# A two-layer mixer and feed-forward step on one core: the modulation vectors as 32-column float32 products on TensorE inside the mixers

## The chip, the cores and the metric

The kernel runs on one NeuronCore of a Trainium2 chip. The metric is the device time of one execution in microseconds; the kernel before takes 1740.79 us (median of three runs, 1739.17 to 1743.87). Engines are named as in the profile: PE is TensorE's matrix product, PEld its weight load, DVE VectorE, ACT ScalarE, POOL GpSimd, SP the engine whose queue issues most loads.

## The reference

One step of a hybrid backbone with two layers over 640 tokens (512 latent, 128 context) of width 1024. Cut to what matters here:

```python
def trunk_layer(x, mod, s0, prm, l, pool_seg):
    sh1, sc1, g1, sh2, sc2, g2 = jnp.split(mod, 6, axis=-1)
    h = rmsnorm(x, prm['norm1_g'][l]) * (1 + sc1) + sh1
    cols = jnp.einsum('bnd,de->bne', h, prm['w_in'][l])
    ...                       # gated DeltaNet, chunked MLP, pooling
    x = x + g1 * mix
    h = rmsnorm(x, prm['norm2_g'][l]) * (1 + sc2) + sh2
    gate, up = jnp.split(jnp.einsum('bnd,df->bnf', h, prm['w_gu'][l]), 2, axis=-1)
    x = x + g2 * jnp.einsum('bnf,fd->bnd', silu(gate) * up, prm['w_down'][l])

# for the context tokens (c_ctx) and for the latent tokens (c), in each layer:
mod = jnp.einsum('bd,de->be', jax.nn.silu(c), w_mod[l]) + b_mod[l]     # 6144 numbers
```

The part that changes is `mod`: for each of two layers a product of two vectors of 1024 numbers (context and latent) with a matrix of 1024 x 6144 float32 numbers, 25 MB a layer.

## The kernel before

Tokens lie in the free dimension, features on the 128 partitions. Every large product runs in float32r with both operands split in a high and a low part, so one block of 128 x 128 weights takes three matmuls of 320 (or 322) columns: `xhi,wh`, `xlo,wh` and `xhi,wl` (`mm3`, line 117 through the helper `mm`). A weight tile `w` of 8 row blocks comes by SP, is split by ACT (line 322), DVE (line 122) and POOL (line 326), and serves two halves of 320 tokens (`gemm_xs`, or `gemm_act` for the output and down projections).

A layer has four stages. **The mixer**: 22 weight tiles of the input projection, and between them the DeltaNet of two pairs of heads, each with short convolutions, decay matrices (`prep`), an inverse by substitution (`inverse`, whose 15 steps are products with `selr`, each waiting for DVE) and a scan over five chunks (`chain`, products on `R` and `S` with DVE steps between). **The output projection**: 8 tiles, each followed by the residual `x` and the scaled split `xhi`, `xlo` for the next norm. **The feed-forward part**: 22 pairs of gate and up products in three pieces, each piece followed by 8 tiles of the down projection.

**The modulation.** The first two sixths of layer 0 (shift and scale of the first norm) are made at the start by `first_mod` on PE: `sc` holds the two condition vectors as 32 columns per row block, and four row blocks run side by side on different column groups of the array (`tile_position=(0, 32 g)`), each a float32 product of 512 moving columns of `w_mod`. Four transposes and a reduction then give the columns. The other ten sixths of both layers are 160 **steps** of 512 columns x 128 rows each (`pump_`): DVE multiplies and adds for the one condition (line 125, `ma<-wm,sc,ma`), ACT multiplies for the other (line 150, `wm<-wm,sc`) and POOL adds (line 282). After 8 steps `mod_sums` adds over the partitions: with 8 transposes on PE and two DVE reductions in layer 0's mixer and output projection, with DVE transposes and four tiny products (`ms,quarters`) in the feed-forward part. Steps are put behind halves of products: by the table `PUMPS` in layer 0's mixer (32 of them by its end), one behind each half in the output projection and in the feed-forward part. All 160 are done by 802 us; layer 1 has none in its output projection or its feed-forward part, and none in its mixer. The load of a step (256 KB) is issued three steps ahead (`WM` = 3) by SP.

**The order.** Instructions have priorities in the order of the program, with offsets from the table `PRI` (`at(...)`); a scheduler makes from these a fixed order on each engine, and each engine runs its own order strictly. PSUM tiles for the small products (`md`) come from a ring of two, shared by the modulation, the transposes of `row_sums` and others.

Of the kernel before, what the change touches and what calls it, by code (L numbers as in the profile page):

```python
# [16 lines left out]
D = 1024  # L17
# [14 lines left out]
POUT = 1  # L32
# steps of the modulation after each half of a product, by branch
PUMPS = {'log0': (0, 0), 'k00': (0, 0), 'q00': (1, 2), 'sgu0': (1, 1), 'z0': (0, 1), 'v10': (1, 1), 'q10': (0, 0), 'v00': (1, 0), 'k10': (0, 1), 'pool0': (1, 0)}
# [11 lines left out]
def host_constants():  # L46
# [10 lines left out]
    # from here on: not kept on chip as they are  # L57
# [34 lines left out]
def tile_hybrid_step(ctx: ExitStack, tc: tile.TileContext,  # L92
# [59 lines left out]
    class at:  # L152
        """the instructions inside come that much earlier in the order of issue"""
# [23 lines left out]
    def in_turn(key, ins):  # L177
        """instructions of one kind in the order of the program"""
# [29 lines left out]
    quarters = const.tile([P, 32], F32, name="quarters")  # L208
# [10 lines left out]
    # steps: 512 columns x 128 rows of w_mod; a step's load is issued some steps ahead of its arithmetic  # L219
    SIXTHS = [(0, 2), (0, 4), (0, 3), (0, 5), (1, 1), (1, 0), (1, 2), (1, 4), (1, 3), (1, 5)]  # L220
    steps = [(l, w * D + c0, k) for l, w in SIXTHS for c0 in (0, 512) for k in range(KT)]
    ps_ = {"i": 0, "j": 0, "ma": None, "wm": {}, "due": None, "at": "mix0"}

    def mod_sums(l, c0, ma):
        t0 = c0 // P
        if ps_["at"] != "ffn0":
            for s in range(2):
                pt = md()
                for cb in range(4):
                    nc.tensor.transpose(pt[:, cb * P:(cb + 1) * P], ma[:, s, cb * P:(cb + 1) * P], ident)  # L230
                m = mod[:, l, s, t0:t0 + 4]
                nc.vector.tensor_reduce(m, pt.rearrange("p (c n) -> p c n", c=4), op=ADD, axis=AX.X)
                tt(m, m, bmod[:, l, t0:t0 + 4], ADD)
            mod_scales(l, c0)
            return
        # sums over the 32 rows of each quarter, then over the quarters
        ms = sm.tile([P, 2, 16], F32, tag="ms", name="ms", bufs=1)
        for s in range(2):
            pt = md()
            nc.vector.transpose(pt, ma[:, s])  # L240
            nc.vector.tensor_reduce(ms[:, s], pt.rearrange("p (c n) -> p c n", n=32), op=ADD, axis=AX.X)
        pt = md()
        for a in range(4):
            mm(pt[32 * a:32 * a + 32, 0:8], quarters, ms.rearrange("p s (t a) -> p a s t", a=4)[:, a], True, True, tile_position=(0, 32 * a))
        tt(mod[:, l, :, t0:t0 + 4], pt[:, 0:8].rearrange("p (s t) -> p s t", s=2),
           bmod[:, l, t0:t0 + 4].unsqueeze(1).to_broadcast([P, 2, 4]), ADD)
        mod_scales(l, c0)
# [5 lines left out]
    def pump(n=1):  # L253
        with at("pump"):
            pump_(n)

    def pump_(n):
        for _ in range(n):
            if ps_["due"] is not None:
                mod_sums(*ps_["due"])  # L260
                ps_["due"] = None
            i = ps_["i"]
            if i >= len(steps):
                return
            while ps_["j"] < min(len(steps), i + WM):
                l, c0, k = steps[ps_["j"]]
                wm = wp.tile([P, 512], F32, tag="wm", name="wm", bufs=WM)
                nc.sync.dma_start(wm, w_mod[l, k * P:(k + 1) * P, c0:c0 + 512])
                ps_["wm"][ps_["j"]] = wm
                ps_["j"] += 1  # L270
            l, c0, k = steps[i]
            wm = ps_["wm"].pop(i)
            if k == 0:
                ps_["ma"] = sm.tile([P, 2, 512], F32, tag="ma", name="ma", bufs=1)
            ma = ps_["ma"]
            if k == 0:
                behind_recent("v", ts, ma[:, 0], wm, sc[:, k, 0:1], None, MUL)
                behind_recent("a", times, f"pump{ps_['at']}", ma[:, 1], wm, sc[:, k, 1:2], "a")
            else:
# [3 lines left out]
            if k == KT - 1:  # L283
                ps_["due"] = (l, c0, ma)
            ps_["i"] += 1

    def pump_to(l, w):
        """until that sixth of the modulation is there"""
        n = 2 * KT * (SIXTHS.index((l, w)) + 1)
        while ps_["i"] < n:  # L290
            pump()
        if ps_["i"] == n and ps_["due"] is not None:
            mod_sums(*ps_["due"])
            ps_["due"] = None

# [1 line left out]
    def wload(parts, kn, n):  # L297
        """parts: [(dram [rows, n], k0, kn)] -> [P, kn, n]"""
# [7 lines left out]
    def wsplit(v):  # L306
        """hi, lo as blocks [P, n]"""
# [32 lines left out]
    def mmk(o, wb, k, xk, sl):  # L340
        """one k block of the products with the scaled residual; 16 columns: hi and lo in one operand"""
# [47 lines left out]
    class Norm:  # L389
        """scaled residual split in two, and the row statistics of the plain one."""  # L390
# [33 lines left out]
        def rstd(self, after=None):  # L424
            """per row: [row in chunk, chunk]"""
# [30 lines left out]
    wsp = tc.alloc_tile_pool(name="wsh", bufs=1, side="right")  # L456
    with tc.tile_pool(name="xin", bufs=1) as xp:
# [27 lines left out]
        def first_w(pool, j, c0, kp=KT):  # L485
            """512 columns of w_mod; the row blocks from kp on in the tiles of the later steps"""
# [950 lines left out]
```

## Time and profile before

| | |
|---|---|
| median of three runs | 1740.79 us (1739.17 to 1743.87) |
| profiled execution, first to last instruction | 1737.7 us |
| PE busy, PEld busy | 1666.4 us (96%), 1603.2 us (92%) |
| DVE, ACT, POOL busy | 1155.2 us (66%), 761.1 us (44%), 585.3 us (34%) |
| mean granted PE clock | 0.987 of full |

The page gives no other time of the profiled execution than this span. Busy times of PE are to be read with care: a matmul of 320 columns is shown with 0.31 us, while in dense stretches the next one starts 0.15 us after it, so short waits disappear behind the modelled ends.

### The profile page before, as it was taken

How to read it: one execution, taken by the hardware profiler on the slowest of the kernel's cores; microseconds unless marked ns; L12 is line 12 of the kernel's file. 1: busy time of each engine (PE TensorE's matmuls, PEld its weight loads, DVE VectorE, ACT ScalarE, POOL GpSimd, SP SyncE). 2: the span in 40 equal slices, each digit the busy share in tenths (PEclk: the TensorE clock that was granted, in tenths of full speed). 3: DMA queues.
4: the chain of work that ended last, by engine and by line, in shares of the span. 5: the costliest groups of instructions: out<-in, count | busy, mean ns of one | idle time of the engine just before them, and what ended most of it. 6: DMA issues, size and time to landing. Idle time of an engine off the chain costs nothing.

```text
span 1737.7 us, 33153 instructions
## 1 busy us (share of the span) xinstructions
PE 1666.4 (96%) x12952; PEld 1603.2 (92%) x12952; DVE 1155.2 (66%) x2462; ACT 761.1 (44%) x1564; POOL 585.3 (34%) x578
## 2 busy tenths in 40 slices
PE   6999999998899999999999999999999999999997
PEld 4788989988899999999998899999999999999997
DVE  6698688799888688877467777675544434433454
ACT  4557765554444344434246656543322212321232
POOL 3342330367645454554164112013411221222110
PEclk8999999999999999999999999999999999999999
DMA  9431231444444544453241211113222222222221
GB/s 316 143 98 57 68 99 29 150 127 139 145 141 141 154 137 143 143 158 103 62 144 52 62 38 50 37 51 126 83 73 74 79 79 74 74 73 73 74 85 61
DMA packets 243379, 174.34 MB, mean 100 GB/s; under 512 B 10006, under 2 KB 212376, under 8 KB 243224
## 3 DMA queue, kind: packets, MB, share of 16 engines
q1 hardware_dynamic: 231888, 157.44, 29.8%
q10 hardware_dynamic: 10184, 12.29, 2.2%
q0 software_dynamic: 1152, 2.51, 0.4%
q8 instruction: 102, 1.67, 0.4%
q14 instruction: 53, 0.43, 0.1%
HBM read 163.29 MB, written 8.91 MB: 99 GB/s over the span
## 4 chain that ended last, share of the span: by engine, by line
PE 53%; DVE 3%; ACT 1%; issue 1%; POOL 0%; DMA 0%; DVEq 0%; POOLq 0%; ACTq 0%
PE acc L117 47%; PE dl L117 5%; DVE wl L122 0%; PE md L117 0%; DMA w<-in_w_down_dram 0%; PE dl L1379 0%; DVE cv L125 0%; POOL guh L830 0%; PE md L760 0%; DVE yt L125 0%; DVE st L125 0%; DVE Z L122 0%; ACT wh L322 0%; ACT MT L945 0%; DVE SI L122 0%
## 5 line engine op out<-in xcount | busy, mean ns | idle before, releaser
L117 PE MATMUL acc<-xhi,wh 128*128 128x322 f32 (+2 forms) x2112 | 667.4, 316 | 5.4 <-DVE ga L122 4.6
L117 PE MATMUL acc<-xlo,wh 128*128 128x322 f32 (+2 forms) x2112 | 666.0, 316 | 1.4 <-DVE xlo L125 1.2
L117 PE MATMUL acc<-xhi,wl 128*128 128x320 f32 (+1 forms) x2080 | 655.0, 315 | 5.1 <-DVE wl L122 5.1
L326 POOL TENSOR_TENSOR wl<-w,wh 128x384 fp32r<-128x384 f32 x188 | 258.7, 1376 | 792.5 <-ACT wh L322 777.9
L117 PEld LDWEIGHTS acc<-xhi,wh 128*128 128x128 f32 (+1 forms) x2112 | 399.4, 189 | 10.7 <-PE acc L117 7.2
L117 PEld LDWEIGHTS acc<-xlo,wh 128*128 128x128 f32 (+1 forms) x2112 | 400.2, 189 | 4.1 <-POOL spp L1148 1.5
L117 PEld LDWEIGHTS acc<-xhi,wl 128*128 128x128 f32 x2080 | 396.4, 191 | 6.6 <-DVE wl L122 5.9
L322 ACT CAST wh<-w 128x1024 fp32r<-128x1024 f32 (+1 forms) x188 | 194.5, 1035 | 343.4 <-PE acc L117 282.6
L282 POOL TENSOR_TENSOR ma<-ma,wm 128x512 f32<-128x512 f32 x140 | 207.2, 1480 | 133.5 <-ACT wm L150 113.8
L122 DVE TENSOR_TENSOR wl<-w,wh 128x640 fp32r<-128x640 f32 (+1 forms) x188 | 213.3, 1134 | 50.5 <-ACT wh L322 23.9
L117 PE MATMUL acc<-ah,wh 128*128 128x320 f32 (+2 forms) x632 | 195.6, 309 | 0.7 <-ACT ah L1322 0.7
L117 PE MATMUL acc<-al,wh 128*128 128x320 f32 (+2 forms) x632 | 195.1, 309 | 0.1
L117 PE MATMUL acc<-ah,wl 128*128 128x320 f32 (+2 forms) x632 | 195.1, 309 | 0.0
L150 ACT ACTIVATE wm<-wm,sc 128x512 f32<-128x512 f32 x140 | 101.1, 723 | 135.0 <-DVE ma L125 117.8
L125 DVE SCALAR_TENSOR_TENSOR x<-acc,mod,x 128x128 f32<-128x128 f32 (+3 forms) x192 | 77.9, 434 | 119.8 <-PE acc L117 119.5
L125 DVE SCALAR_TENSOR_TENSOR ma<-wm,sc,ma 128x512 f32<-128x512 f32 x140 | 134.9, 964 | 25.6 <-DMA wm<-in_w_mod_dram 24.7
L117 PEld LDWEIGHTS acc<-ah,wh 128*128 128x128 f32 x632 | 118.7, 188 | 1.2 <-ACT ah L1322 1.1
L117 PEld LDWEIGHTS acc<-al,wh 128*128 128x128 f32 x632 | 118.7, 188 | 0.3 <-DVE al L122 0.3
L117 PEld LDWEIGHTS acc<-ah,wl 128*128 128x128 f32 x632 | 118.7, 188 | 0.0
L1322 ACT CAST ah<-ga 128x320 fp32r<-128x320 f32 x88 | 40.5, 460 | 155.9 <-DVE ga L125 155.9
L150 ACT ACTIVATE ga<-ga,bt 128x320 f32<-128x320 f32 x132 | 57.4, 468 | 89.9 <-DVE ga L122 89.9
L122 DVE TENSOR_TENSOR ga<-acc,rst 128x320 f32<-128x320 f32 x88 | 42.4, 483 | 73.9 <-PE acc L117 73.4
(369 smaller groups left out, 2481.7 us busy)
## 6 DMA issues: line engine op xcount, KB each, us to landing
w<-in_w_gu_dram SPq DMA_DIRECT2D x88, 512.0 KB, 3.7
wm<-in_w_mod_dram SPq DMA_DIRECT2D x162, 256.0 KB, 2.9
w<-in_w_in_dram SPq DMA_DIRECT2D x44, 512.0 KB, 3.6
w<-in_w_down_dram SPq DMA_DIRECT2D x32, 512.0 KB, 4.2
w<-in_w_out_dram SPq DMA_DIRECT2D x32, 256.0 KB, 3.0
wf<-in_w_mod_dram SPq DMA_DIRECT2D x30, 256.0 KB, 6.5
w<-in_w_down_dram SPq DMA_DIRECT2D x16, 384.0 KB, 3.4
x<-xd ACTq DMA_DIRECT2D x16, 320.0 KB, 4.7
```

Of the source, the lines that this page charges most:

```text
L117: return nc.tensor.matmul(o, lhsT=l, rhs=r, start=st, stop=sp, **kw).ins
L122: recent["v"] = nc.vector.tensor_tensor(o, a, b, op=op).ins
L125: recent["v"] = nc.vector.scalar_tensor_tensor(o, a, s, b, op0=op0, op1=op1).ins
L150: recent["a"] = nc.scalar.activation(o, i, f, **kw).ins
L282: nc.gpsimd.tensor_tensor(ma[:, 1], ma[:, 1], wm, op=ADD)
L322: nc.scalar.copy(wh, v)
L326: nc.gpsimd.tensor_tensor(wl[:, c:], v[:, c:], wh[:, c:], op=SUB)
L1322: nc.scalar.copy(hi[:, sl], ga[:, sl])
```

## The change

All ten later sixths are computed as the first two were, on PE. A **group** is 512 columns and four row blocks (512 rows); there are 40. Its four products (`mm(pm[g:g+32], sc[:, k], w)`, 128 x 32 weights, 512 moving float32 columns) go to four column groups of one PSUM tile, DVE copies the tile to `msb`, and four float32 products with `msb` as weights and two columns of the constant `I16` add the four row groups up; one DVE addition per group then makes `mod`. `first_mod` does the same in place of its transposes. The steps on DVE, ACT and POOL and both forms of `mod_sums` are gone. A group is issued for each full unit of a running sum that grows by `SHARE` behind every half of an input projection: 0.6 in layer 0's mixer, 0.45 in layer 1's; so 27 groups stand in layer 0's mixer and 13 in layer 1's, and none in the output projections and feed-forward parts. `WM` becomes 4: the four loads of the next group are issued as the four products of this one free their tiles.

```diff
-POUT = 1
-PUMPS = {'log0': (0, 0), 'k00': (0, 0), 'q00': (1, 2), 'sgu0': (1, 1), ...
+SHARE = (0.6, 0.45)
...
-W32, WM, WHL = 2, 3, 2
+W32, WM, WHL = 2, 4, 2
...
+    groups = [(l, w * D + c0, k0) for l, w in SIXTHS for c0 in (0, 512) for k0 in (0, 4)]
...
+    def mod_columns(ws, l, c0, k0, msb):
+        pm = md()
+        for i, w in enumerate(ws):
+            g = 32 * (i % 4)
+            mm(pm[g:g + 32, :], sc[:, k0 + i, :], w, i < 4, i >= len(ws) - 4, tile_position=(0, g))
+        copy("msb", msb, pm, "v")
+        pt = md()
+        for cb in range(4):
+            mm(pt[:, 2 * cb:2 * cb + 2], msb[:, cb * P:(cb + 1) * P], C("I16")[:, 0:2], True, True)
+        m = mod[:, l, :, c0 // P:c0 // P + 4]
+        tt(m, pt[:, 0:8].rearrange("p (t s) -> p s t", s=2),
+           bmod[...] if k0 == 0 else m, ADD)
...
+    def mod_loads():
+        while ps_["j"] < min(4 * len(groups), 4 * ps_["i"] + WM):
+            ...
+            wm = wp.tile([P, 512], F32, tag="wm", name="wm", bufs=WM)
+            nc.sync.dma_start(wm, w_mod[l, k * P:(k + 1) * P, c0:c0 + 512])
...
+    def pump(share):
+        ps_["sum"] += share
+        while ps_["sum"] >= 1.0 - 1e-6:
+            ps_["sum"] -= 1.0
+            if ps_["i"] < len(groups):
+                pump_group()      # mod_loads, mod_columns, mod_scales, mod_loads
...
-                behind_recent("v", stt, ma[:, 0], wm, sc[:, k, 0:1], ma[:, 0], MUL, ADD)
-                behind_recent("a", times, f"pump{ps_['at']}", wm, wm, sc[:, k, 1:2], "a")
-                nc.gpsimd.tensor_tensor(ma[:, 1], ma[:, 1], wm, op=ADD)
...
-    def gemm_xs(wb, xs, evac, pumps=(1, 1), done=None):
+    def gemm_xs(wb, xs, evac, share=0.0, done=None):
...
-            pump(pumps[half])
+            pump(share)
...
-    def gemm_act(wb, ks, xs, evac, n=1):
+    def gemm_act(wb, ks, xs, evac):
...
-            pump(n)
...
-                gemm_xs(wcol(C_Z + h * P, P), xs, ev_act(zs[h], AF.Silu), PUMPS.get(f"z{l}", (0, 1)))
+                gemm_xs(wcol(C_Z + h * P, P), xs, ev_act(zs[h], AF.Silu), SHARE[l])
```

What this does to the order is seen at three places. **PE, layer 0's first inverse.** `dl<-S,selr` are the steps of the substitution, each waiting for DVE; `acc<-x` are the products of the input projection that stand between them. Before:

```order
L117 MATMUL acc<-xhi,wl 128x322
L117 MATMUL dl<-S_986,selr 128x320 x2
L117 MATMUL acc<-xhi,wh 128x322
L117 MATMUL acc<-xlo,wh 128x322
L117 MATMUL acc<-xhi,wl 128x322
```

and of the changed kernel, where `md<-wm,sc` are the products of a group and `md<-cst,msb` the four small ones:

```order
L116 MATMUL md<-cst,msb 128x2 x4
L116 MATMUL md<-wm,sc 32x512 x2
L116 MATMUL dl<-S_1051,selr 128x320 x3
L116 MATMUL md<-wm,sc 32x512
L116 MATMUL acc<-xhi,wl 128x322
L116 MATMUL acc<-xhi,wh 128x322
L116 MATMUL acc<-xlo,wh 128x322
L116 MATMUL dl<-S_1051,selr 128x320 x3
L116 MATMUL md<-wm,sc 32x512
```

The four products of this group stand at three places, with full-width matmuls between them. Over the program the 160 products of the 40 groups stand in 69 such unbroken runs, 51 in layer 0's mixer and 18 in layer 1's: 18 of four, 15 of three, 6 of two and 30 alone (the listing has one more of three, the tail of `first_mod`'s).

**DVE, layer 0's output projection.** `x` is the residual, `xlo` the split for the next norm, `wl` the low part of a weight tile, `ma` the accumulator of a modulation step. Before:

```order
L125 SCALAR_TENSOR_TENSOR x_4330<-acc,mod,x_4330 128x192
L125 SCALAR_TENSOR_TENSOR x_4330<-acc,mod,x_4330 128x128
L125 SCALAR_TENSOR_TENSOR ma<-wm,sc,ma 128x512
L125 SCALAR_TENSOR_TENSOR xlo<-x_4330,sc_79,xhi 128x512
L125 SCALAR_TENSOR_TENSOR xlo<-x_4330,sc_79,xhi 128x128
L122 TENSOR_TENSOR wl<-w_4542,wh 128x640
```

Changed:

```order
L124 SCALAR_TENSOR_TENSOR x_4717<-acc,mod,x_4717 128x192
L124 SCALAR_TENSOR_TENSOR x_4717<-acc,mod,x_4717 128x128
L121 TENSOR_TENSOR wl<-w_4873,wh 128x640
L124 SCALAR_TENSOR_TENSOR xlo<-x_4717,sc_79,xhi 128x512
L124 SCALAR_TENSOR_TENSOR xlo<-x_4717,sc_79,xhi 128x128
```

The modulation steps between residual and split are gone, and the split of the next weight tile has moved ahead of `xlo`.

**SP, layer 0's mixer.** `w` are weight tiles of the input projection (512 KB), `wm` loads of `w_mod` (256 KB). Before:

```order
L303 DMA w_2658<-in_w_in_dram 128x8x128
L268 DMA wm<-in_w_mod_dram 128x512 x5
L303 DMA w_2731<-in_w_in_dram 128x8x128
L268 DMA wm<-in_w_mod_dram 128x512 x3
L303 DMA w_2865<-in_w_in_dram 128x8x128
```

Changed:

```order
L282 DMA w_3180<-in_w_in_dram 128x8x128
L246 DMA wm<-in_w_mod_dram 128x512 x16
L282 DMA w_3285<-in_w_in_dram 128x8x128
L246 DMA wm<-in_w_mod_dram 128x512 x12
L282 DMA w_3370<-in_w_in_dram 128x8x128
```

Up to four groups' loads now stand in a row ahead of a weight tile. Each of them waits until a product of the group before has run on PE; before, it waited for POOL or ACT.

## Rows read from the trace of the kernel before

**Rows 1.** Busy time per engine (us, share of the span, instructions), from the page.

```profile
PE 1666.4 (96%) x12952; PEld 1603.2 (92%) x12952; DVE 1155.2 (66%) x2462; ACT 761.1 (44%) x1564; POOL 585.3 (34%) x578
```

**Rows 2.** Busy time by stretch; first column window and length, count in brackets, then clock, DMA.

```profile
core 0: us, PE busy (x) PEld busy (x) DVE busy (x) ACT busy (x) POOL busy (x), PEclk, DMA share, GB/s
51.00:353.00 302.00, 286.18 (x2791) 268.44 (x2789) 238.43 (x620) 188.73 (x456) 92.49 (x116) 0.98 0.28 85
353.00:427.00 74.00, 65.74 (x410) 62.55 (x411) 68.93 (x100) 35.70 (x55) 53.69 (x48) 0.95 0.41 126
427.00:603.00 176.00, 168.75 (x1150) 166.09 (x1149) 145.13 (x217) 75.16 (x114) 100.02 (x70) 0.99 0.49 148
603.00:780.00 177.00, 174.59 (x1214) 171.97 (x1213) 145.23 (x220) 74.22 (x112) 94.80 (x66) 1.00 0.47 143
916.00:1200.00 284.00, 277.88 (x2766) 261.78 (x2765) 199.76 (x583) 165.02 (x409) 53.47 (x83) 1.00 0.19 57
1200.00:1258.00 58.00, 57.20 (x382) 55.70 (x382) 35.27 (x67) 22.52 (x35) 30.44 (x30) 1.00 0.27 82
1258.00:1424.00 166.00, 166.00 (x1125) 166.00 (x1124) 68.34 (x135) 41.25 (x64) 33.59 (x24) 1.00 0.25 74
1424.00:1594.00 170.00, 170.00 (x1152) 170.00 (x1150) 69.39 (x136) 42.27 (x64) 35.49 (x24) 1.00 0.26 75
```

**Rows 3.** Chain of waits in layer 1's mixer: shares by engine and line, pieces in time.

```profile
by line: PE acc L117 46.2%; PE dl L117 26.8%; issue 2.6%; PE md L117 2.4%; DVE wl L122 2.2%; DVE cv L125 2.1%; POOL guh L830 1.7%; PE md L760 1.7%; DVE yt L125 1.4%; DVE Z L122 1.2%; ACT MT L945 1.1%; DVE SI L122 0.9%; PE md L1117 0.8%; ACT
...
958.12 0.59 DVE ZT L125 x2
958.71 1.58 DVE cv L125
```

**Rows 4.** The same columns as in rows 2, of the tile `ma` alone, layer 0's mixer.

```profile
51.00:353.00 302.00, 4.53 (x32) 3.72 (x32) 28.68 (x32) 3.55 (x5) 40.09 (x28) 0.98 0.28 85
```

**Rows 5.** Instructions on the modulation tiles `wm`: count, ns min/median/max, first and last start.

```profile
L125 DVE SCALAR_TENSOR_TENSOR ma<-wm,sc,ma x140: 735/751/1869, 82.3 to 800.9; 128x512 f32<-128x512 f32 x140
L150 ACT ACTIVATE wm<-wm,sc x140: 705/724/758, 89.1 to 801.7; 128x512 f32<-128x512 f32 x140
L282 POOL TENSOR_TENSOR ma<-ma,wm x140: 1262/1335/1945, 103.5 to 802.6; 128x512 f32<-128x512 f32 x140
...
L147 DVE COPY wm<-md x2: 690/690/691, 46.1 to 50.2; 128x512 f32<-128x512 f32 x2
```

**Rows 6.** Timeline of PE: eight products of `first_mod` among wide matmuls.

```profile
43.84 0.30 PE L117 MATMUL acc<-xhi,edT 128*128 128x320 f32 x1
44.07 1.92 PE L117 MATMUL md<-wf,sc 128*32 128x512 f32 x16
45.93 0.41 PE L117 MATMUL dl<-xhi,eon 128*128 128x320 f32 x1
46.18 0.31 PE L117 MATMUL dl<-xlo,eon 128*128 128x320 f32 x1
...
46.77 1.02 PE L117 MATMUL dl<-ss,cst 128*128 128x512 f32 x2
47.64 0.60 PE L508 MATMUL md<-r_ident,wm 128*128 128x128 f32 x4
```

**Rows 7.** Timeline of PE: small float32 products, each with its own 128 columns of weights.

```profile
69.49 0.33 PE L117 MATMUL dl<-g,cst 128*128 128x20 f32 x2
...
70.56 0.38 PE L117 MATMUL dl<-g,cst 128*128 128x20 f32 x2
70.78 0.40 PE L117 MATMUL acc<-xhi,eon 128*128 128x322 f32 x1
```

**Rows 8.** DMA issues from the page: count, KB each, median us from issue to landing.

```profile
wm<-in_w_mod_dram SPq DMA_DIRECT2D x162, 256.0 KB, 2.9
...
wf<-in_w_mod_dram SPq DMA_DIRECT2D x30, 256.0 KB, 6.5
```

More of the change, by code (lines that the diff above doesn't have):

```diff
@@ L207, in tile_hybrid_step @@
     ident = rr["ident"].bitcast(F32)
-    quarters = const.tile([P, 32], F32, name="quarters")
     selr = const.tile([P, 15, P], F32R, name="selr")
@@ L220, in tile_hybrid_step @@
     SIXTHS = [(0, 2), (0, 4), (0, 3), (0, 5), (1, 1), (1, 0), (1, 2), (1, 4), (1, 3), (1, 5)]
[L221 to L241, printed above, removed]
-        pt = md()
[L243 to L247, printed above, removed]
+    groups = [(l, w * D + c0, k0) for l, w in SIXTHS for c0 in (0, 512) for k0 in (0, 4)]
+    ps_ = {"i": 0, "j": 0, "wm": [], "sum": 0.0}
+    def mod_columns(ws, l, c0, k0, msb):
[4 more added lines that the diff above has]
+        copy("msb", msb, pm, "v")
+        pt = md()
+        for cb in range(4):
+            mm(pt[:, 2 * cb:2 * cb + 2], msb[:, cb * P:(cb + 1) * P], C("I16")[:, 0:2], True, True)
+        m = mod[:, l, :, c0 // P:c0 // P + 4]
+        tt(m, pt[:, 0:8].rearrange("p (t s) -> p s t", s=2),
+           bmod[:, l, c0 // P:c0 // P + 4].unsqueeze(1).to_broadcast([P, 2, 4]) if k0 == 0 else m, ADD)
     def mod_scales(l, c0):
@@ L251, in mod_scales @@
             mod_scale(l, 0 if c0 < 2 * D else 1)
-    def pump(n=1):
-        with at("pump"):
[L255 to L261, printed above, removed]
-            i = ps_["i"]
[L263 to L279, printed above, removed]
-                behind_recent("v", stt, ma[:, 0], wm, sc[:, k, 0:1], ma[:, 0], MUL, ADD)
-                behind_recent("a", times, f"pump{ps_['at']}", wm, wm, sc[:, k, 1:2], "a")
-                nc.gpsimd.tensor_tensor(ma[:, 1], ma[:, 1], wm, op=ADD)
-            if k == KT - 1:
-                ps_["due"] = (l, c0, ma)
-            ps_["i"] += 1
@@ L287, in pump_to @@
-    def pump_to(l, w):
[L289 to L294, printed above, removed]
+    def mod_loads():
+        while ps_["j"] < min(4 * len(groups), 4 * ps_["i"] + WM):
+            l, c0, k = groups[ps_["j"] // 4]
+            k += ps_["j"] % 4
+            wm = wp.tile([P, 512], F32, tag="wm", name="wm", bufs=WM)
+            nc.sync.dma_start(wm, w_mod[l, k * P:(k + 1) * P, c0:c0 + 512])
+            ps_["wm"].append(wm)
+            ps_["j"] += 1
@@ new lines, in pump_group @@
+    def pump_group():
+        with at("pump"):
+            i = ps_["i"]
+            l, c0, k0 = groups[i]
+            mod_loads()
+            ws = [ps_["wm"].pop(0) for _ in range(4)]
+            mod_columns(ws, l, c0, k0, sm.tile([P, 512], F32, tag="msb", name="msb", bufs=1))
+            if k0:
+                mod_scales(l, c0)
+            ps_["i"] += 1
+            mod_loads()
+    def pump(share):
[4 more added lines that the diff above has]
+                pump_group()
@@ L297, in wload @@
+    def pump_to(l, w):
+        while ps_["i"] < 4 * (SIXTHS.index((l, w)) + 1):
+            pump_group()
     def wload(parts, kn, n):
@@ L499, in first_mod_ @@
         def first_mod_(ws, c0, pool):
-            pm = md()
-            for k in range(KT):
-                g = 32 * (k % 4)
-                mm(pm[g:g + 32, :], sc[:, k, :], ws[k], k < 4, k >= KT - 4, tile_position=(0, g))
-            msb = pool.tile([P, 512], F32, tag="msb", name="msb", bufs=1) if pool else wm_tile()
-            copy("msb", msb, pm, "v")
-            pt = md()
-            for cb in range(4):
-                nc.tensor.transpose(pt[:, cb * P:(cb + 1) * P], msb[:, cb * P:(cb + 1) * P], ident)
-            m = mod[:, 0, :, c0 // P:c0 // P + 4]
-            nc.vector.tensor_reduce(m, pt.rearrange("p (cb g m) -> p m cb g", cb=4, g=4)[:, 0:2], op=ADD, axis=AX.X)
-            tt(m, m, bmod[:, 0, c0 // P:c0 // P + 4].unsqueeze(1).to_broadcast([P, 2, 4]), ADD)
+            mod_columns(ws, 0, c0, 0, sm.tile([P, 512], F32, tag="msb", name="msb", bufs=1))
         mark("mod00")
@@ L557, in tile_hybrid_step @@
                 tt(dst.rearrange(v, w=64), pt.rearrange(v, w=64), e, ADD)
-        nc.vector.tensor_reduce(quarters, ident.rearrange("p (g m) -> p m g", g=4), op=ADD, axis=AX.X)
         p1 = dl()
@@ L573, in tile_hybrid_step @@
             xk = xks[k]
-            if k % 2:
-                sq = xp.tile([P, NT], F32, tag="sq", name="sq", bufs=1)
-            else:
-                sq = sm.tile([P, 2, 512], F32, tag="ma", name="sq", bufs=1).rearrange("p s n -> p (s n)")[:, 0:NT]
+            sq = xp.tile([P, NT], F32, tag="sq", name="sq", bufs=2)
             if k < 2:
@@ L647, in gemm_in @@
                 wb, done = early.pop(c0, None) or (wcol(c0, n), None)
-                gemm_xs(wb, xs, evac, PUMPS.get(f"{key}{l}", (0, 1)), done)
+                gemm_xs(wb, xs, evac, SHARE[l], done)
             def cwt(name, tag):
@@ L1137, in pool @@
                 for i in range(2):
-                    gemm_xs(wcol(C_PP + i * P, P), xs, ev_act(pT[i], AF.Identity), PUMPS.get(f"pool{l}", (0, 1)))
+                    gemm_xs(wcol(C_PP + i * P, P), xs, ev_act(pT[i], AF.Identity), SHARE[l])
                 pn = zs[1:4]
@@ L1171, in branches @@
                 for i in range(2):
-                    gemm_xs(wcol(C_VB + i * P, P), xs, ev_act(vT[i], AF.Gelu_apprx_tanh), PUMPS.get(f"sgu{l}", (0, 1)))
+                    gemm_xs(wcol(C_VB + i * P, P), xs, ev_act(vT[i], AF.Gelu_apprx_tanh), SHARE[l])
                 vg = qT[0:2] + vn[0:1]
@@ L1196, in branches @@
                 for i in range(2):
-                    gemm_xs(wcol(C_U + i * P, P), xs, ev_act(uT[i], AF.Gelu_apprx_tanh), PUMPS.get(f"sgu{l}", (0, 1)))
+                    gemm_xs(wcol(C_U + i * P, P), xs, ev_act(uT[i], AF.Gelu_apprx_tanh), SHARE[l])
                 for gp in range(2):
@@ L1288, in ft @@
                 return ftp.tile([P, NT], F32, tag="ft", name=name, bufs=4)
-            ps_["at"] = f"out{l}"
             pump_to(l, 2)
@@ L1296, in tile_hybrid_step @@
                 wb = wblock([(w_out[l, 4 * P:8 * P, cs], 0, 4), (w_out[l, 0:4 * P, cs], 4, 4)], 8, P)
-                gemm_act(wb, range(8), yb + ya, resid(l, 16, n, x[n]), POUT)
+                gemm_act(wb, range(8), yb + ya, resid(l, 16, n, x[n]))
                 nrm.add(n, x[n], ft("sq"), shift=False)
@@ L1304, in tile_hybrid_step @@
             mark(f"ffn{l}")
-            ps_["at"] = f"ffn{l}"
             pieces = (8, 8, 6)
```

1 line of the change is left out of this document (removed).

## The prediction

> **What bounds the kernel now.** The page first: PE is busy 96% of the span and its weight loads 92%, DVE 66% [rows 1]. That is an average over stages, so the table by stretch comes next [rows 2]. Its rows go in pairs, layer 0 against layer 1: the two mixers (51 to 353 and 916 to 1200), the stretch from the first residual to the first gate (353 to 427 and 1200 to 1258), and the first two pieces of the feed-forward part (427 to 603 and 603 to 780; 1258 to 1424 and 1424 to 1594). In layer 1's feed-forward part PE is busy all the time: it is the bound there. In layer 0's the same matmuls take longer, DVE is busy some 145 us of 176 instead of 68 of 166, and the work that layer 1 lacks is the modulation steps. In the mixers the busy time hides short waits, so I read the chain of waits over layer 1's mixer [rows 3]: PE's pieces are 46.2 + 26.8 + 2.4 + 1.7 + 0.8 = 78% of it. The other 22%, 62 us of 284, are steps of DVE, ACT and POOL that PE waits for, each of 0.6 to 1.6 us as in the two pieces shown. The chain isn't traced back into layer 0; the same share of its 302 us is 66 us. So the mixers are nearer to a PE bound than to any other, and PE's time is what the change spends.
>
> **The change part by part.** *Gone outside the mixers.* Without steps layer 0 can run as layer 1 does, so I take the differences of the pairs [rows 2]: 74 - 58 = 16, 176 - 166 = 10 and 177 - 170 = 7, together -33 us. The idle time of PE shown there (8.3, 7.2 and 2.4 us) bounds it from the other side at -18; a loss is excluded, since nothing is added there. The steps in the third piece are few and are put at nothing.
>
> *Gone in layer 0's mixer.* 32 transposes of `ma` on PE [rows 4], some 0.1 us each: -3 us. On DVE 28.7 us of steps and sums go [rows 4] and 27 copies of 0.69 us [rows 5] with 27 small additions come, some 23 us: a gain of 6 us on an engine that is busy 79% [rows 2]. On ACT and POOL whole steps of 0.72 and 1.34 us go [rows 5], but PE seldom waits for these. I put all this relief, with the slightly better clock of a denser PE (0.98 there, 1.00 later [rows 2]), at -6 us; from 0 to -20.
>
> *The large products.* Eight of them, two groups back to back and two passes each, stand among wide matmuls in `first_mod` [rows 6]. The matmul before starts at 43.84 and would be followed 0.15 us later, at 43.99; the next wide one starts at 45.93 and holds 0.25 us instead of 0.15. So eight products cost 45.93 - 43.99 + 0.10 = 2.04 us. A float32 product of 512 columns over the full width, alone, takes 47.64 - 46.77 = 0.87 us [rows 6]. So four side by side take the time of one, 0.86 us, and what is left, 2.04 - 2 x 0.86 = 0.32 us, is the change of the array's division in and out. This decides the term: four products cost 0.86 us only if they stand together. In the changed order they stand in 69 unbroken runs, and a run of one costs as much as a run of four. 69 x (0.86 + 0.32) = 81 us; if the split did not matter and the change of division cost nothing, 40 x 0.86 = 34 us. I take 81, since both parts are read from rows of the same instruction.
>
> *The small products.* Each takes `msb` as weights, 128 columns, in two passes. The nearest rows are float32 products of 20 columns with 128 columns of weights [rows 7]: 12 passes from 69.49 to 70.78, 0.1075 us each, whatever the few columns. 40 groups x 4 products x 2 passes x 0.1075 = 34 us. The Trainium skill, "TensorEngine Tiling (Array Packing)", Performance Considerations, states an overhead of about 60 cycles for a matmul, one of a single column being as long as one of 60. By that, 25 ns at 2.4 GHz (an estimate), the 320 passes would cost 8 us and the sum below would be 26 us lower. The trace shows four times as much for each pass here [rows 7], and I go by that. In `first_mod` the small products take the place of transposes and a reduction: +1 us.
>
> *What PE's waits cover.* An added run is free as far as PE would have waited there. At most that is the whole 22%, 62 + 66 = 128 us; at least nothing. 45 of the 69 runs stand within a few rows of a step of the inverses or of the scans, where PE waits for others; the other 24 stand in the dense products of the input projection. A run of 1.18 us in a wait of 0.6 us (the shorter piece shown [rows 3]) covers 0.6: 45 x 0.6 = 27 us. I take -27, and not more, since a free stretch at the wrong place covers nothing.
>
> *New waits.* PE waits in its order for the four loads, for the copy on DVE and for one of two `md` tiles. A load takes 2.9 us alone and 6.5 us in a row of many [rows 8]; the four of a group can start only when the four products before have run. The closest groups stand 2 to 5 us of PE work apart, some ten of 40, and wait 1 us or less each, one some 3 us. Up to 16 of these loads stand ahead of a weight tile on SP, but that tile is first used 20 us of PE's work or more behind the products that they wait for, so nothing is late there. The copy of 0.69 us has 1 to 2 us of other PE work over it. I take +8 us; from 0 to +32 (0.8 us for each group).
>
> *The sum:* -33 - 3 - 6 + 81 + 34 + 1 - 27 + 8 = +55 us. Against the execution's own span of 1737.7 us that is 1793 us; the median of the runs shown lies 3 us above the span, so 1796 us.
>
> **The rivals.** *PE's waits swallow the products* (faster). The 115 us of new PE work fill the 128 us of the chain that are not PE's, the mixers stay as long as they are, and what remains is -33 - 6: about 1702 us. For it: the groups may go anywhere, and a scheduler places them. Against it: 24 runs stand in dense stretches, and gemm rows were there to fill the waits before and did not. It decides from a cover of 82 us on (55 + 27), about two thirds of the 128. *The idle time of the weight loads is what can be filled*: in the mixers PE's loads are busy 268 of 302 and 262 of 284 us [rows 2], so 34 + 22 = 56 us are free for the products instead of 27, and the time is 1767 us. For it: a delayed product also delays others that would have waited, and a wait at one place is made up at the next; against it are the 24 runs in dense stretches. The Trainium skill, "Perfetto Trace Analysis", Identifying the Most-Contended Engine, says just this: PE's headroom is judged by the busy share of its weight loads, not by that of the matmuls. *The products are cheaper than their rows*: if a run of one costs a quarter of a run of four, the runs cost 34 us and the changes of division, 69 x 0.32 = 22, instead of 81, and the time is 1771 us; short passes that cost nothing would give 1762. Against it are the lone product of 0.87 us [rows 6] and the passes of 0.1075 us [rows 7]. *The groups wait for their copies, loads and tiles*: 0.8 us for each group, and nothing of the runs is covered; 1796 + 24 + 27 = 1847 us. For it: DVE is busy 79% of layer 0's mixer and runs the copies in its order.
>
> **How the numbers follow.** The forecast, 1796 us, has a chance of 0.50; the loads' idle time filled 0.17, cheaper products 0.11, the waits of the groups 0.13, all swallowed 0.09. The range of 8 in 10 runs from 1755, below the filled loads and the cheaper products, to 1830, half-way into the long waits; it leaves out the faster case and part of the slowest. A difference under 0.3%, 5 us, cannot be told from no change. Faster has the 0.09 of the swallowing rival, less the part that ends within 5 us: 0.08; the same 0.04; slower 0.88.
>
> **What would show it.** In the changed profile the stretch from the first residual to the first gate of layer 0 should take 58 to 60 us and the first two pieces 166 and 170. Layer 0's mixer should be some 50 us longer, with layer 1's some 25 to 30 longer, and the chain there PE's to more than 80%. A product alone between wide matmuls should hold PE for 0.86 us and 0.3 more, and the four small ones 0.86 us. If the mixers grow by less than 30 us together, the cover was taken too small and the forecast is wrong on its main term; if the chain names DVE's copy or the loads of `wm`, the waits were.

## The result and the profile after

The changed kernel takes 1817.13 us (median of four runs, 1810.56 to 1819.37); the kernel before, on the same chip, 1739.98 us. The ratio is 1.0436, interval 1.0409 to 1.0463: slower by 77 us. The forecast of 1796 us had the sign and the range of 1755 to 1830 holds the time, but 21 us were missing. The profiled execution's span is 1814.4 us against 1737.7.

Busy time per engine of the changed kernel, from its page, answers [rows 1]:

```profile
PE 1764.2 (97%) x13448; PEld 1642.4 (91%) x13448; DVE 943.3 (52%) x2283; ACT 647.3 (36%) x1398; POOL 391.3 (22%) x438
```

DVE lost 212 us of work, ACT 114 and POOL 194, and the kernel is slower: PE gained 98. Busy time by stretch of the changed kernel, in the columns of [rows 2]: layer 0's mixer, first residual to first gate, the first two pieces of its feed-forward part, layer 1's mixer.

```profile
55.00:425.00 370.00, 362.96 (x3198) 296.30 (x3196) 216.88 (x631) 162.19 (x418) 57.80 (x90) 0.99 0.39 122
425.00:483.00 58.00, 57.17 (x380) 55.67 (x381) 35.18 (x66) 22.22 (x34) 29.35 (x29) 1.00 0.25 74
483.00:649.00 166.00, 166.00 (x1125) 166.00 (x1124) 68.42 (x134) 41.57 (x65) 33.86 (x24) 1.00 0.25 74
649.00:820.00 171.00, 171.00 (x1158) 171.00 (x1157) 69.69 (x138) 42.29 (x64) 34.90 (x24) 1.00 0.26 75
...
956.00:1277.00 321.00, 311.82 (x2959) 278.66 (x2958) 210.53 (x609) 161.15 (x406) 54.69 (x84) 0.99 0.28 87
```

Against [rows 2] the three stretches behind the mixer became what layer 1 has (58, 166 and 171 us), as forecast. The mixers grew, and PE is idle 7 us of 370 in the one and 9 of 321 in the other, where it was idle 16 of 302 and 6 of 284.

The same by landmarks of the traces: the first start of `lgT` (the mixer's first product is out), of the residual `x`, and of the gate `ga` in each piece. The columns e1, e5 and e8 are experiments told below; e1 is the kernel without any of the 40 groups, so the floor under both.

| us | before | after | e1, no groups | e5, dense | e8, mixed |
|---|---|---|---|---|---|
| start to layer 0's `lgT` | 51.4 | 55.4 | 53.7 | 53.1 | 53.1 |
| layer 0's mixer | 302.2 | 370.3 | 282.3 | 307.5 | 299.8 |
| residual to gate | 74.2 | 57.6 | 57.5 | 58.0 | 64.4 |
| feed-forward, piece 1 | 175.9 | 166.2 | 166.2 | 186.9 | 180.7 |
| piece 2 | 176.1 | 170.3 | 170.3 | 192.5 | 176.5 |
| piece 3 to layer 1's `lgT` | 136.9 | 136.3 | 135.8 | 154.4 | 136.9 |
| layer 1's mixer | 283.7 | 321.2 | 283.8 | 283.5 | 284.7 |
| the rest, to the last instruction | 537.4 | 537.2 | 537.0 | 537.0 | 537.7 |

The chain of waits in layer 1's mixer, shares by engine and line, answers [rows 3]:

```profile
by line: PE acc L116 41.5%; PE dl L116 24.0%; PE md L116 10.7%; issue 1.9%; PE md L723 1.8%; POOL guh L793 1.7%; ACT jk L149 1.4%; DVE yt L124 1.0%; DVE SI L121 0.9%; PE md L1080 0.9%; DMA x<-xd 0.8%; DVE so L124 0.8%; DVE Z L121 0.8%; DVE 
```

PE's pieces are 79%, as before (78%), and the other 21% of 321 us are 67 us against 62. By itself that doesn't settle what was covered, because, as shown below, time of the chain on other engines is mostly not idle time of PE. The timeline of PE shows what a group costs, answering [rows 6]; `x4` are two products of a group side by side, `x2` is one (each is recorded as two passes):

```profile
78.57 0.31 PE L116 MATMUL acc<-xlo,eon 128*128 128x322 f32 x1
78.81 1.05 PE L116 MATMUL md<-wm,sc 128*32 128x512 f32 x4
79.79 0.56 PE L116 MATMUL acc<-xhi,eon 128*128 128x322 f32 x2
80.19 0.32 PE L116 MATMUL acc<-xlo,eon 128*128 128x322 f32 x1
80.34 0.46 PE L116 MATMUL acc<-xhi,eon 128*128 128x322 f32 x2
80.73 1.04 PE L116 MATMUL md<-wm,sc 128*32 128x512 f32 x2
81.71 0.42 PE L116 MATMUL acc<-xlo,eon 128*128 128x322 f32 x1
81.96 0.32 PE L116 MATMUL acc<-xhi,eon 128*128 128x322 f32 x1
```

Two products hold PE from 78.81 to 79.79, one alone from 80.73 to 81.71: 0.98 us each. The start is some 0.09 us late and the next wide matmul keeps 0.10 us more than its 0.15 (81.71 to 81.96), so an unbroken run of one or two costs 1.17 us, the forecast's 1.18. Four side by side, in e5 below, hold PE for 1.00 us, so the number of products in a run hardly matters. In the trace the 69 runs are 19 of four, 14 of three, 6 of two and 30 alone, which makes the 160 products; the counts given with the change make 159.

### The profile page after: what moved, and what is told of

It reads as the page before. It is cut to its first block, busy times and chain, and to the rows that moved or that the text cites. A ratio compares the mean times of both kernels' runs of the same rounds, so it can differ in the third digit from the quotient of the medians.

```text
span 1814.4 us, 33318 instructions
## 1 busy us (share of the span) xinstructions
PE 1764.2 (97%) x13448; PEld 1642.4 (91%) x13448; DVE 943.3 (52%) x2283; ACT 647.3 (36%) x1398; POOL 391.3 (22%) x438
## 4 chain that ended last, share of the span: by engine, by line
PE 83%; DVE 4%; ACT 1%; issue 1%; DMA 1%; POOL 1%; DVEq 0%; ACTq 0%; POOLq 0%
PE acc L116 68%; PE dl L116 8%; PE md L116 5%; PE md L723 0%; DVE yt L124 0%; DVE wl L121 0%; POOL guh L793 0%; PE dl L1340 0%; DMA w<-in_w_down_dram 0%; PE md L1080 0%; ACT wh L301 0%; ACT jk L149 0%; DMA wm<-in_w_mod_dram 0%; DVE xlo L124 0%; PE md L769 0%
## 5 line engine op out<-in xcount | busy, mean ns | idle before, releaser
L305 POOL TENSOR_TENSOR wl<-w,wh 128x384 fp32r<-128x384 f32 x188 | 270.5, 1439 | 1133.6 <-ACT wh L301 1055.5
L121 DVE TENSOR_TENSOR wl<-w,wh 128x640 fp32r<-128x640 f32 (+1 forms) x188 | 193.0, 1027 | 45.1 <-ACT wh L301 44.2
L341 DVE COPY bt<-acc 128x2 f32<-128x2 f32 (+1 forms) x134 | 21.2, 158 | 132.1 <-PE acc L116 131.9
L116 PE MATMUL md<-wm,sc 128*32 128x512 f32 x326 | 76.5, 604 | 1.2 <-DMA wm<-in_w_mod_dram 1.0
L121 DVE TENSOR_TENSOR up<-acc,rst 128x320 f32<-128x320 f32 x88 | 42.8, 486 | 59.2 <-PE acc L116 59.2
```

What stands on the lines that cost most here:

```text
L116: return nc.tensor.matmul(o, lhsT=l, rhs=r, start=st, stop=sp, **kw).ins
L121: recent["v"] = nc.vector.tensor_tensor(o, a, b, op=op).ins
L305: nc.gpsimd.tensor_tensor(wl[:, c:], v[:, c:], wh[:, c:], op=SUB)
L341: nc.vector.tensor_copy(bt, o[:, 0:2])
```

## The experiments

Ratios are against the kernel before on the same chip. Theory A stands throughout for: a group costs PE's whole time, wherever it stands.

**e1: no groups.** All later sixths of the modulation are the bias alone.

```diff
     def pump_group():
+        ps_["i"] += 1
+        return
...
+                nc.vector.tensor_copy(mod[:, l_, s_, 8 * w_:8 * w_ + 8], bmod[:, l_, 8 * w_:8 * w_ + 8])
```

> The changed kernel without its 40 groups: no loads of w_mod, no products, no copies for them; the ten later sixths of the modulation are the bias alone. What is left is the floor under both kernels. Theory A (the groups cost PE's whole time, 69 x 1.18 + 40 x 0.86 = 115 us, nothing of it lies in waits, and 4 us come from the loads): 1817 - 119 = 1698 us, which is also the kernel before less the 42 us that the prediction took off for the steps; the two mixers 302 - 9 = 293 and 284 us. Theory B (the prediction's: 27 us of the products lie in waits, 8 us are new waits): 1817 - (115 - 27 + 8) = 1721 us, so that the steps would have cost only 19 us. Theory C (the weight loads' idle time, 56 us, covers): 1817 - 59 = 1758 us, above the kernel before.

Measured 1689.01 us, ratio 0.9711 (0.9693 to 0.9729). The groups cost 128 us, more than theory A's 119 and far from B and C; the steps of the kernel before cost 51 us, not 42. The stage table says where the 51 were: 19.9 in layer 0's mixer, 16.7 behind it, 9.7, 5.8 and 1.1 in the three pieces, less some 2 us at the start, where this kernel has the new `first_mod`. Some 12 of the 51 us are the granted clock: [rows 2] has 0.98, 0.95 and 0.99 in layer 0's mixer, the stretch behind it and the first piece, where e1 has 1.00. Without steps the two mixers are alike (282.3 and 283.8). Their stretches in this floor, in the columns of [rows 2]:

```profile
54.00:336.00 282.00, 274.97 (x2765) 260.56 (x2765) 195.20 (x572) 160.60 (x417) 54.91 (x90) 1.00 0.19 54
866.00:1150.00 284.00, 277.81 (x2766) 261.57 (x2764) 200.02 (x584) 164.36 (x408) 53.47 (x83) 1.00 0.20 57
```

PE is shown idle 7.0 and 6.2 us there: 13 us in both mixers is what could have been covered, waits so short that they disappear behind the modelled ends of the matmuls aside.

**e2: the four products of a group side by side.** The one whose load lands last is queued first, the other three behind it at a high priority: 40 unbroken runs instead of 69.

```diff
-        for i, w in enumerate(ws):
+        for i in (3, 2, 1, 0):
...
+            behind(ins, prev)
```

> The four products of a group are queued so that they stand side by side: the product of the load that lands last comes first, the other three right behind it. 40 unbroken runs of four instead of 69 of one to four; all else is as in the changed kernel. Theory A (a run costs 1.18 us however few products it holds, and nothing of it is covered): 29 runs x 1.18 = 34 us less, 1783 us, plus 0 to 8 us if waiting for the last load costs something. Theory B (0.6 us of a run is covered): 29 x 0.58 = 17 us less, 1800 us. Theory D (a lone product costs a quarter, a split group costs only the changes of the array's division): 29 x 0.32 = 9 us less, 1808 us; if lone products filled waits for nothing: 1817 us or more.

Measured 1787.72 us, ratio 1.0279 (1.0255 to 1.0303): 29.4 us less than the changed kernel for 29 runs less. That is past the 17 of B and the 9 of D and close to the 34 of A. What PE waited for from 54 to 1260 us (total, times, longest):

```profile
PE md L116 <- DMA wm<-in_w_mod_dram: 11.8, 9, 2.2
PE dl L116 <- POOL guh L799: 4.2, 7, 1.9
```

The products now wait 11.8 us for the last load, which they did for 1.0 us in the changed kernel; the missing 5 us may have gone there, or into the clock, which was at its lower level for 27 us of the two mixers in this trace and for 14 in that of the changed kernel. A product alone is not a quarter of a group, and a split group pays a whole run more.

**e3: as e2, without the small products.** DVE adds columns of the copied tile instead, so the row groups aren't summed.

```diff
+        if len(ws) == 4:
+            tt(m, msb[:, 0:8].rearrange("p (t s) -> p s t", s=2), ...)
+            return
```

> As the run with the four products together, but the 40 groups have no small products: the vector engine's addition reads eight columns of the copied tile instead (so the row groups are not added up). 160 products or 320 passes less. Theory A (0.1075 us a pass, nothing covered): 34 us below the run with the four together, 1749 us where that is 1783. The note's 25 ns a pass: 8 us below it. Were they covered by waits: 0.

Measured 1759.4 us, ratio 1.0106 (1.0085 to 1.0127): 28.3 us below e2 for 320 passes, 0.088 us each. The row that was used gave 0.1075 [rows 7]. The difference is uncertain by some 6 us; in the two profiled executions it is 32 us. The estimate of 25 ns a pass from the Trainium skill, "TensorEngine Tiling (Array Packing)", Performance Considerations, would have given 8 us; the overhead of 60 cycles doesn't carry over to these passes, whose price was read better from the nearest row.

**e4: no large products.** A quarter of the loads stays, and the tile that the small products read is copied straight from the load.

```diff
+        if len(ws) == 1:
+            copy("msb", msb, ws[0], "v")
```

> The changed kernel without the four large products of its 40 groups: one load of 256 KB a group is copied on the vector engine straight to the tile that the small products read. What goes is 69 runs on PE and three quarters of the loads of w_mod; copies, small products and additions stay. Theory A: 1817 - 81 = 1736 us, or some 4 us less for the loads that nobody waits for, 1732; the floor run plus 34 us. Theory B (27 us of the runs were covered): 1817 - 54 - 8 = 1755 us.

Measured 1741.91 us, ratio 1.0008 (0.9996 to 1.002): 75.2 us less than the changed kernel, 1.09 for each of 69 runs. Theory B's 62 is too little. But the floor plus 34 us would be 1723: there are 19 us more here than the small products explain. Some 10 of them are the granted clock, which never fell in the floor's mixers and fell four times in these (columns of [rows 2]):

```profile
54.00:369.00 315.00, 304.05 (x2983) 287.64 (x2982) 212.78 (x632) 167.23 (x422) 54.71 (x90) 0.99 0.26 77
900.00:1201.00 301.00, 293.01 (x2854) 276.71 (x2854) 205.06 (x608) 165.33 (x409) 55.82 (x83) 0.98 0.21 60
```

It was at its lower level for 6.8 us in the first and 13.7 in the second; half of that is lost. So an excess nearly as large as the changed kernel's (22 us, below) comes without the large products.

**e5: other places.** As e2, but 12 groups in layer 0's mixer, 28 in the feed-forward part, where PE never waits, none in layer 1's mixer.

```diff
-SHARE = (0.6, 0.45)
+SHARE = (0.27, 0.0)
+FSHARE = (0.32, 0.0)
...
-... xs2, evu)
+... xs2, evu, FSHARE[l])
```

> The four products of a group side by side as before (1787.7 us), but other places: 12 groups in layer 0's mixer (a share of 0.27) and 28 in layer 0's feed-forward part (a share of 0.32 behind each half of its gate and up products), where PE never waits in the floor run; none in layer 1's mixer. It asks whether the mixers' waits cover anything of a group. In the mixers the 40 groups cost 352.4 - 282.3 = 70.1 and 317.0 - 283.8 = 33.2 us over the floor run, 2.6 us each. Theory A (no cover anywhere; a group costs 1.18 + 0.86 = 2.04 us of PE's time, and what is above it in the mixers are waits and clock): the feed-forward part grows by 28 x 2.04 = 57 us from 472.3 us, the mixer by 12 x 2.6 = 31, sum 1689 + 88 = 1777 us. Theory B (a run has 0.6 us covered in the mixers): the mixers' 2.6 us are cheaper than a dense stretch, a group costs 3.2 us there and the time is 1689 + 31 + 90 = 1810 us.

Measured 1777.05 us, ratio 1.0211 (1.0197 to 1.0226), where theory A said 1777 and B 1810. That the number is met to the microsecond is luck, as theory A's two terms missed in opposite ways. The stage table: 28 groups cost 61.5 us in the feed-forward part (57 expected), 2.2 each; 12 cost 25.2 us in the mixer (31 expected), 2.1 each. The stretches of the three pieces:

```profile
419.00:606.00 187.00, 186.67 (x1279) 176.91 (x1279) 75.38 (x156) 41.28 (x64) 33.26 (x23) 1.00 0.39 120
606.00:798.00 192.00, 191.34 (x1312) 180.02 (x1314) 76.91 (x158) 42.21 (x64) 34.92 (x24) 1.00 0.40 121
798.00:952.00 154.00, 150.81 (x1027) 139.78 (x1020) 77.35 (x159) 45.15 (x76) 46.96 (x52) 1.00 0.44 134
```

A group costs the same where PE never waits (idle 0.3 and 0.7 us in the first two) as in the mixer: on average the mixer covers nothing. Of its 12 groups two stand at the steps of the second inverse and four among the products of the scans, too few to price one kind of place alone. All 40 groups together are 88 us over the floor, 40 x 2.2. One group in the dense stretch, four products (`x8` passes) side by side:

```profile
497.53 0.31 PE L117 MATMUL acc<-xhi,wl 128*128 128x322 f32 x1
497.76 1.07 PE L117 MATMUL md<-wm,sc 128*32 128x512 f32 x8
498.76 0.41 PE L117 MATMUL acc<-xhi,wh 128*128 128x320 f32 x1
```

**e6: the copy on ACT.**

```diff
-ENG = {..., "msb": "v", ...}
+ENG = {..., "msb": "a", ...}
```

> The run with the four together (1787.7 us) with the copy of a group's sums on the scalar engine instead of the vector engine, which runs its queue in order and stands still until the products before the copy have run. Theory A (the excess of 2.6 over 2.04 us a group, 22 us, comes from the clock and from waiting for the last load): no change, 1785 to 1791 us. Theory W (the vector engine's queue standing still behind the copy is the new wait): up to 15 us less, 1773 us.

Measured 1797.47 us, ratio 1.0324 (1.031 to 1.0338), 10 us above e2. The mixers took 352.3 and 314.2 us against 352.4 and 317.0 in e2: DVE's queue behind the copy was not what PE waited for. The loss lies at the start, 61.7 us against 54.0. `first_mod`'s copies went to ACT as well, which the expectation had overlooked, and PE waits 8.8 us for them there, where it waited 5.2 for DVE's in e2; the clock was also at its lower level for twice as long (27 us against 14).

**e7: one sixth on PE, in the kernel before.** The shift of layer 0's second norm by four groups in the output projection instead of 16 steps.

```diff
-POUT = 1
+POUT = 0
...
+                if l == 0 and n in (0, 2, 4, 6):
+                    pump_group()
```

> The kernel before with one sixth of the modulation changed: the shift of layer 0's second norm, whose 16 steps stood in the output projection, is made by four groups on PE there, each with its four products together; all other steps stay where they were. The output projection took 74.2 us with the steps and 57.5 in the floor run, 16.7 us for 16 steps. Theory A: they go and four groups of 2.04 us come, 8.2 us: 1740 - 8.5 = 1731.5 us. Rival: the groups' copies and additions hold the vector engine as the steps did, and nothing is gained: 1740 us.

Measured 1745.17 us, ratio 1.003 (1.0018 to 1.0042): a loss of 4 us where a gain of 8.5 was expected. The stretch from residual to gate took 78.0 us, not 66. Its busy time, PE's waits in it, and the steps (`ma<-wm,sc,ma`) that ran by 440 us (duration in ns min/median/max, first and last start):

```profile
354.00:432.00 78.00, 70.62 (x471) 64.46 (x471) 56.24 (x97) 29.56 (x44) 41.19 (x40) 0.97 0.47 145
```

```profile
PE dl L117 <- DVE ss L122: 2.8, 1, 2.8
PE acc L117 <- DVE xlo L125: 2.2, 1, 2.2
```

```profile
L125 DVE SCALAR_TENSOR_TENSOR ma<-wm,sc,ma x13: 739/752/1796, 405.9 to 438.5; 128x512 f32<-128x512 f32 x13
```

The scheduler drew the feed-forward part's first steps forward, to 405.9 us, where DVE has the last `xlo` and the norm's `ss` to make, and PE waited for those. In this stretch the rival's price came true and more, by another cause than the copies: the steps that were taken out made room for others on the same engine. The first piece, which had fewer steps left, took 171.9 us instead of 175.9, so the 3.8 us lost here came back there. The profiled execution is 3.5 us longer than that of the kernel before, and the stage times put this at the start (1.7 us) and in layer 1 (1.6 and 0.8), where the edit changes nothing; that part isn't explained.

**e8: layer 0's first three sixths on PE.** As e7, with no steps in the mixer either: eight groups in its last input projections (half a group behind each half of a product there), four in the output projection; 112 steps stay in the feed-forward part.

```diff
-PUMPS = {'log0': (0, 0), ..., 'pool0': (1, 0)}
+PUMPS = {}
...
+    GP = [(0, 2), (0, 4), (0, 3)]
```

> As the run before, with the gate and the scale of layer 0's first half done the same way: no steps in layer 0's mixer either (they cost 302.2 - 282.3 = 19.9 us over the floor run), but eight groups in its last, dense input projections, and four in the output projection; the 112 steps of the feed-forward part stay, where they cost 17 us. Theory A: 1740 - 19.9 - 16.7 + 12 x 2.04 = 1728 us. Rival (a group costs 2.6 us in the mixer wherever it stands): 1732 us; if the feed-forward part's steps cost more when all of them are left to it: 1740 us.

Measured 1732.92 us, ratio 0.9947 (0.9933 to 0.996): faster than both kernels. Eight groups cost 17.5 us in the mixer and four 6.9 behind it, together 24.4 us or 2.0 each (the products of the first of the four stand 2 us ahead of the boundary). The scheduler put one of the eight beside the second inverse and one into the scan. The feed-forward part's steps start behind it this time, and its first piece pays 5 us more than before. Residual to gate, and the first two pieces:

```profile
353.00:417.00 64.00, 63.16 (x433) 58.85 (x432) 41.91 (x73) 22.06 (x34) 27.69 (x31) 1.00 0.41 128
417.00:598.00 181.00, 174.44 (x1175) 171.37 (x1174) 148.75 (x224) 79.48 (x121) 103.70 (x73) 0.97 0.49 149
598.00:774.00 176.00, 173.22 (x1192) 170.94 (x1192) 143.44 (x215) 74.15 (x112) 93.55 (x66) 1.00 0.48 144
```

**e9: the steps spread thinner.** None behind the first tile, then 0.82 a half.

```diff
+        if thin["on"]:
+            thin["sum"] += 0.82 * n
```

> The run e8 (1732.9 us) with the 112 steps of the feed-forward part spread thinner: none behind the first tile, then 0.82 of a step behind each half instead of one, so that they reach into the third piece, which had almost none. In e8 the three pieces took 180.7, 176.5 and 136.9 us against 166.2, 170.3 and 135.8 in the floor run, 21.8 us for 112 steps, 14.5 of them in the first piece. Theory A (the first steps hold the vector engine while the first tiles of the part need it, and a thinner row of steps is hidden): the first two pieces lose 8 to 10 us, the third gains 2, 1726 us. Rival (a step costs its 0.2 us wherever it stands, or the third piece, which splits the next norm as the output projection does, pays as that did, 1 us a step): 1733 to 1745 us.

Measured 1736.8 us, ratio 0.9982 (0.9973 to 0.999), 4 us worse than e8: the three pieces took 182.0, 173.3 and 142.2 us. The second gained 3, the third lost 5, and the first, whose steps came later, gained nothing. So the third piece is no free place, as the rival had it, and what the first piece loses isn't settled.

## Why the prediction was right, and where it was off

The terms of the sum, against what the runs give for each:

| term | predicted | measured | from |
|---|---|---|---|
| outside the mixers | -33 | -32.7 | stage table, 16.6 + 9.7 + 5.8 + 0.6 |
| steps gone from layer 0's mixer | -9 | -19.9 | before against e1 |
| large products | +81 | +75.2 | after against e4 |
| small products | +34 | +28.3 | e2 against e3 |
| start | +1 | +4.0 | stage table |
| cover, new waits, clock | -19 | +21.8 | what is left of 76.7 |

The range held partly by luck: the last line is 41 us above its forecast, and layer 0's mixer and both kinds of products are 22 us below theirs.

**Right.** Layer 0 without steps runs as layer 1 does, to 0.1 us in the first two pieces. The runs' price, one run of one as dear as one of four, holds in the timeline (0.98 us for one product and for two, 1.00 for four) and in e2 (29.4 us for 29 runs). The small products' price from the nearest row held to 0.02 us a pass.

**The step that failed: "What PE's waits cover".** It took the 22% of the chain that are not PE's, 62 + 66 = 128 us, as time in which PE waits, and a wait of 0.6 us as cover for each of 45 runs. The chain doesn't say that. It follows dependencies, and while a link runs on DVE, PE can be busy with other work. PE's timeline over the two pieces that were quoted, 958.12 to 960.29 [rows 3], in the kernel before:

```profile
958.12 0.31 PE L117 MATMUL acc<-xhi,wl 128*128 128x322 f32 x1
958.27 0.31 PE L117 MATMUL acc<-xhi,wh 128*128 128x322 f32 x1
958.41 0.31 PE L117 MATMUL acc<-xlo,wh 128*128 128x322 f32 x1
...
959.77 0.31 PE L117 MATMUL acc<-xlo,wh 128*128 128x322 f32 x1
959.92 0.31 PE L117 MATMUL acc<-xhi,wl 128*128 128x322 f32 x1
960.07 0.31 PE L117 MATMUL acc<-xhi,wh 128*128 128x320 f32 x1
960.22 0.31 PE L117 MATMUL acc<-xlo,wh 128*128 128x320 f32 x1
960.58 0.41 PE L117 MATMUL dl<-S,selr 128*128 128x320 f32 x1
```

PE starts a product every 0.15 us through both pieces; of the 2.2 us it lost 0.2, from 960.22 to 960.58. The idle time was in [rows 2] all along, 15.8 and 6.1 us, and the text set it aside as hidden behind modelled ends. In the floor e1 it is 13 us for both mixers as shown. The products used none of it: idle is 7.0 and 9.2 us in the changed kernel, and e5 shows the same 2.1 to 2.2 us a group in the mixer and in the dense stretch. With a cover of zero the sum would have been 1823.

**Mis-sized the other way: the relief of layer 0's mixer**, 19.9 us instead of 9. The forecast counted DVE's balance of 6 us and the transposes. The row already showed it: layer 1's mixer, which does the same work without steps, took 18 us less [rows 2]. The clock alone is 6 to 7 of it (0.98 of 302 us there, 1.00 in e1), as much as the forecast had for all of the relief but the transposes. The pair was used for the three stretches behind the mixer and not for the mixer.

**New waits, and the clock.** The last line of the table is 21.8 us, where +8 was set for waits alone. The granted clock has a part in it. Layer 1's mixer of the changed kernel, in 1 us windows (columns of [rows 2]), with a stretch of layer 0's mixer ahead:

```profile
87.00:91.00 4.00, 4.00 (x20) 3.76 (x20) 3.08 (x10) 2.49 (x8) 2.16 (x3) 0.57 0.00 0
...
975.00:976.00 1.00, 0.66 (x6) 0.39 (x4) 1.00 (x2) 0.36 (x1) 1.00 (x1) 1.00 0.24 45
976.00:977.00 1.00, 0.00 (x0) 0.00 (x0) 1.00 (x2) 0.00 (x0) 1.00 (x2) 1.00 0.91 299
...
979.00:980.00 1.00, 1.00 (x6) 1.00 (x6) 0.00 (x0) 0.00 (x0) 0.61 (x1) 0.50 0.75 190
983.00:984.00 1.00, 1.00 (x6) 0.96 (x6) 0.00 (x0) 0.14 (x2) 0.00 (x0) 0.50 0.00 0
985.00:986.00 1.00, 1.00 (x9) 0.88 (x8) 0.48 (x2) 0.93 (x5) 0.00 (x0) 1.00 0.00 0
```

PE paused from 975.5 to 977.5 us, with its next step held up by POOL, and then ran at 0.50, the lower of its levels (1.2 GHz), until 984.7. The mean over 975 to 985 is 0.66, a loss of 3.4 us; two more falls, at 87 and 155 us, cost 1.7 each. The floor has none from 42 us to its last 6 us. So about 7 of the 21.8 us are the clock. How the rest divides can't be read exactly, since what a run leaves out also moves the clock and the waits: in the two mixers the clock cost 6.8 us in the changed kernel, 10.2 in e4, 13.6 in e2 and 5.1 in e3. Another 7 to 8 are the difference between PE's own rows of the groups (69 runs of 1.11 us with the 0.1 behind them, 40 short sets of 0.87) and the runs that leave a term out. The remaining 7 are spread over waits too small to name, and how they come about stays open. They are not the copy (e6), and hardly the loads, for which PE waits 1.0 us in layer 0's mixer and not at all in layer 1's. The ring of two `md` tiles was not tried.

**The rivals.** *Swallowed by waits* fell with the cover: there were 13 us to swallow in, not 128. *The weight loads' idle time is filled* fell too: it was 21.4 and 22.4 us in the floor, and is 73.7 and 42.3 in the changed kernel, since a run of float32 products holds PE for 0.98 us and one of its weight loads takes 0.11. So the rule of the Trainium skill, "Perfetto Trace Analysis", Identifying the Most-Contended Engine, that PE's headroom is judged by its share of peak arithmetic or by the busy share of its weight loads, gave 56 us here when taken by the second, and the runs found none. In these mixers the share of PE's matmul rows, 98% in the floor, was the better guide. *Cheaper products* fell by e2, e3 and e5. *The groups wait and nothing is covered* was half right: nothing was covered, and the waits were 0.55 us a group instead of 0.8, clock included.

**What was to show it.** The stretches of 58, 166 and 170 us came. The mixers were to grow by 50 and 25 to 30 us and grew by 68.1 and 37.5. A product alone was to hold PE for 0.86 us and 0.3 more and took 0.98 and 0.19. The chain in layer 1's mixer was to be PE's to more than 80% and is to 79%. The sign that the waits were mis-sized, a chain that names the loads of `wm`, came in a small way: in layer 0's mixer it has 4.4 us of them (257.32 to 261.75), while PE, busy with other products, waited 1.0 us.

## What to carry to other kernels

Work that was moved to the engine that bounds the stretch cost its whole issue time here. Before a cover is taken off the sum, look at the distances between that engine's starts in the timeline, not at the shares of other engines in the chain of waits. Products that use a part of the array's columns were paid by the unbroken run: one alone cost what four side by side did, so the order has to keep them together, with all their data there (29 us less in e2, which still waited 11.8 us for loads). And move only what is dear where it stands: 48 steps cost 37 us in layer 0's mixer and output projection and the other 112 cost 17 us, so taking the first alone to PE made the kernel 0.5% faster (e8), and taking all made it 4% slower.

## What the runs showed of the hardware beyond that

The clock fell without a pause to be seen as well. In the 8 us before 87 us PE is shown busy for 8.00 (modelled ends can hide short pauses), on a mix of single 32-column products, products of 20 columns and the short ones of 2 columns; then the clock was at 0.57 over 4 us. Neither kind of a group's products has to be there for a fall: e4, without the large ones, has falls at 65, 137, 984 and 1086 us, and e3, without the short ones, at 68, 365 and 1000. The kernel without groups (e1) and e5, which has 28 of the 40 in dense stretches and none in layer 1, have none between their start and their end. What brings a fall about was not isolated.
